# Encoder block: a refill's operations ordered behind lower parts of left operands, its first loads four products earlier, and the output weights' sums at other products

## The chip, the core and the metric

The kernel runs on one core of one Trainium2 chip. The metric is the device time of one execution in microseconds. In this core TensorE multiplies, VectorE (DVE) and ScalarE (ACT) work on tiles elementwise, GpSimd (POOL) does the same and issues some transfers, and SyncE (SP) issues most of the DMA transfers from one queue, in order. Each engine runs its instructions in the order in which the program gave them, and waits where an input is not there or a buffer is not free.

## The reference

One layer of an encoder block over 1040 positions (16 learned meta tokens and 1024 others), width 1024, all in float32: one input projection feeds a retention branch and a windowed attention branch, each with a gate and a projection of its own; the two are merged by sigmoid gates, projected once more, normed and added to the input.

```python
u = _rms_norm(h, pre_w)
z = u @ w_in
rq, rk, rv, rg, aq, ak, av, ag, gr, ga = _split_in(z)
...
o_r = o_r * ret_nw.astype(jnp.float32) * jax.nn.silu(rg.astype(jnp.float32))
y_r = o_r.astype(h.dtype) @ w_rb
...
o_a = _windowed_sink_attention(aq, ak, av, sink)[:, META_PAD:].reshape(B, T, ATT_Q)
o_a = o_a * jax.nn.silu(ag.astype(jnp.float32))
y_a = o_a.astype(h.dtype) @ w_ab

mix = jax.nn.sigmoid(gr) * y_r + jax.nn.sigmoid(ga) * y_a
out = mix @ w_o
return h + _rms_norm(out, post_w)
```

## The kernel before

**Precision.** A float32 operand is kept as two tiles: the upper part, cast by ScalarE (names in `h`), and the lower part, the operand less its upper part, made by VectorE in `dve_lo` (L92, names in `l`). A product of two operands is three matmuls in one accumulation (`mm3`, L76 to L78: upper by upper, lower by upper, upper by lower).

**Phases.** After the branches' projections, the retention and the attention come four matrix products, each an instance of `Phase`: z (the gate parts of the input projection, 16 units), r (`w_rb`), a (`w_ab`) and o (`w_out`), four units each. A unit is a strip of 256 columns of weights (phase o: of 256 positions) by 1024 in depth, and it is computed with seven block products in place of eight (the table `PROD`). A product is twelve matmuls with 512 columns: four pieces of the depth by three. The left operands are strips of weights, or sums of their blocks: raw strips `wrz<unit>_<half>` (`wrr`, `wra` in the other phases) are loaded, `prepare` makes the sums (`stz9S` and the like, L1006 and the lines around it), and `split` (L978, L92) casts them into `lhz<unit>_<product>` and `llz<unit>_<product>`, six buffers each. `prepare` runs six products ahead of the product that uses its result (`LEAD = 6`). Results are gathered in tiles `c1`, `u2`, `u3`, `c5` (L1068 is `plus`), multiplied, gated and stored in `z_post` (L1246 to L1260).

**The right operand.** It is kept in big buffers, for each phase the halves B11, T1, B21, B22 and the differences T2, T3, T4, each as an upper and a lower tile (`big0`, `big1`; `T30`, `T31`; `T40`, `T41`). Between two phases `refill` (L1142 to L1194) replaces it: it loads the next phase's matrix in tiles `z000` to `z113` (named for phase, row half, column half and piece; those of the refill behind phase r begin with r), makes differences of them (L1157), and splits each tile into its place as soon as the last product that reads that place is past. A table in `refill` gives each step the number of a product, counted from the end of the phase: at -17 the first loads, at -15 to -12 the first differences, at 0 to 10 the last splits (T3, B22, T4), which lie in the next phase already. A step is issued after the product of its number.

**The output weights' sums.** `pre_load` loads a quarter of `w_out` (`w00k`, `w01k`, `w11k`, `w10k`), and `pre_split` makes four differences of it (L776), casts them (`wT1hk` and so on), makes the lower parts (L92, `wT1lk`) and stores both parts to `preT` (L779, L781), for the refill behind phase a to fetch. `run` hooks them to products of the queue of all phases: the loads of quarter 0, 1, 2 and 3 behind product 16, 28, 40 and 52, the four sums 4, 6, 8 and 10 products later. Phase z has 92 products left at that point of the program, so all quarters lie in z, and the refill's first loads behind product 75.

**Order and buffers.** A scheduler in the framework lays out the instructions of each engine by modelled times and priorities; the order in which the code issues them is one input to it. `tc.issue_after(i)` adds an edge: what is issued under it stands behind instruction `i`. Loads and stores of all this (raw strips, refill, `preT`, gate values `tg_d`) share SP's queue. The staging tiles of the refill and of the sums share two pools: one of seven (the refill's left half-columns, and upper parts of the sums) and one of eight (the refill's right half-columns, the raw quarters and lower parts).

Of the kernel before, what the change touches and what calls it, by code (L numbers as in the profile page):

```python
# [39 lines left out]
def block_kernel(ctx: ExitStack, tc: tile.TileContext, x0, xT, x, meta, w_in, w_rb, w_ab, w_out, post_w,  # L40
# [50 lines left out]
    def dve_lo(o, i, hi):  # L91
        return nc.vector.tensor_tensor(o, i, hi.bitcast(F32), ALU.subtract).ins  # L92
# [19 lines left out]
    def halves_w(u):  # L112
        hi, lo = [], []

        def split(t, act):
            h, l = (wp.tile([P, 4, 256], R, tag=f"w{x}", bufs=4, name=f"w{x}{u}_{len(hi)}") for x in "hl")
            if act:
                nc.scalar.copy(h, t)
            else:
                pool_hi(h, t)  # L120
            hi.append(h)
            lo.append(l)
            return dve_lo(l, t, h)

        return split, ((lambda k, a, b: hi[k // 4][:, k % 4, a:b]), (lambda k, a, b: lo[k // 4][:, k % 4, a:b]))

    def load_w(src, u, act=False):
        split, w = halves_w(u)
        for t in fetch_w(src, u):
            split(t, act)  # L130
        return w
# [25 lines left out]
    def projT(w, c, name, mt=None):  # L157
        wh, wl = w
        a, b = cols(c)
        t = pj(name)  # L160
        if c == 0:
            for k in range(KT):
                nc.tensor.matmul(t[0:48, 0:256], xm[:, k, 0:48], wh(k, 0, 256), start=k == 0, stop=False,
                                 skip_group_check=True)
                nc.tensor.matmul(t[0:NM, 0:256], xm[:, k, 0:NM], wl(k, 0, 256), start=False, stop=k == KT - 1,
                                 skip_group_check=True)
            nc.scalar.copy(mt, t[32:32 + NM, 0:256])
            nc.vector.tensor_tensor(mt, t[0:NM, 0:256], mt, ALU.add)
            return mt
        for k in range(KT):  # L170
            mm3(t[0:b - a, 0:256], xh[k][:, a:b], xl[k][:, a:b], wh(k, 0, 256), wl(k, 0, 256), k == 0, k == KT - 1)
        return t
# [93 lines left out]
    with tc.tile_pool(name="setup", bufs=1, reuse_waits="tile") as st:  # L266
# [87 lines left out]
        split, wv0 = halves_w(U_V)  # L354
# [18 lines left out]
        first = [projT(wv0, 0, "pv0_0", vmeta0), projT(wv0, 1, "pv0_1"), projT(wv0, 2, "pv0_2")]  # L373
# [390 lines left out]
    def pre_load(k, src):  # L764

        w[k] = {}
        for i, j in ((0, 0), (0, 1), (1, 1), (1, 0)):
            w[k][i, j] = t = stage(f"w{i}{j}{k}", 1)
            src(t, 4 * i + k, j)

    def pre_split(k, i, behind):

        n, o, a, b = SUMS[i]
        x = w[k]
        with tc.issue_after(behind):
            nc.vector.tensor_tensor(x[o], x[a], x[b], ALU.subtract)  # L776
        h, l = (stage(f"w{n}{k}{e_}", s, R) for s, e_ in enumerate("hl"))
        nc.scalar.copy(h, x[o])
        nc.sync.dma_start(pre_d[n][0][:, k], h.bitcast(F32))  # L779
        dve_lo(l, x[o], h)  # L780
        nc.sync.dma_start(pre_d[n][1][:, k], l.bitcast(F32))  # L781
        if n == "T4":
            del w[k]

    w, near = {}, []
    gates = [U_G + u for u in range(4)] + [U_AG + u for u in range(4)] + [U_GR + u for u in range(8)]

    def pre_fetch(u):
# [157 lines left out]
    def stage(name, j=0, dt=F32):  # L946
        return (yp if j else lp).tile([P, 512], dt, tag=f"sg{int(j)}", bufs=8 if j else 7, name=name)
# [4 lines left out]
    def split_b(n, k, src):  # L952
        (h, as_), (l, _) = (right(n, s, k) for s in range(2))
        nc.scalar.copy(h, as_(src))
        dve_lo(l, as_(src), h)

    class Phase:
# [18 lines left out]
        def split(self, u, p, src):  # L976
            h, l = (lp.tile([P, 4, P], R, tag=t, bufs=LEAD, name=f"{t}{self.nm}{u}_{p}") for t in ("lh", "ll"))
            nc.scalar.copy(h, src)  # L978
            dve_lo(l, src, h)
            self.ops[u, p] = h, l  # L980

        def prepare(self, u, p):
# [147 lines left out]
    def get_pre(n):  # L1130
        for s in range(2):
            m = B[n][s].shape[1]
            nc.sync.dma_start(B[n][s].bitcast(F32), pre_d[n][s][:, 0:m])
            if m < 4:
                d, as_ = right(n, s, m)
                nc.sync.dma_start(d.bitcast(F32), as_(pre_d[n][s][:, m]))
# [8 lines left out]
    def refill(nm, src):  # L1145

        x = {}

        def load(i, j, ks=range(4)):
            def f():  # L1150
                for k in ks:
                    x[i, j, k] = t = stage(f"{nm}{i}{j}{k}", j)
                    src(t, 4 * i + k, j)
            return f

        def minus(o, a, b):
            return lambda k: nc.vector.tensor_tensor(x[*o, k], x[*a, k], x[*b, k], sub)  # L1157

        def split(n, i, j):
            return lambda k: split_b(n, k, x[i, j, k])  # L1160

        def each(at, n, *fs):
            for k in range(4):
                at.setdefault(n + k if len(fs) > 1 else n + k // 2, []).extend([lambda f=f, k=k: f(k) for f in fs])

        def got(n):
            return lambda: get_pre(n)

        def step(at, n, f):
            for k, j in enumerate(n):  # L1170
                at.setdefault(j, []).append(lambda k=k: f(k))

        if nm == "a":
            at = {-16: [load(0, 0)], -14: [load(1, 1)]}
            each(at, -13, split("B11", 0, 0))
            at.update({-11: [got("T1")], -10: [load(1, 0)], -9: [got("T2")], -5: [got("T3")], -1: [got("T4")]})
            each(at, -7, split("B21", 1, 0))
            each(at, -3, split("B22", 1, 1))
            return at

        at = {-17: [load(0, 0), load(0, 1)], -13: [load(1, 1)], -9: [load(1, 0, range(3))]}
        step(at, (-15, -14, -13, -12), minus((0, 1), (0, 1), (0, 0)))
        step(at, (-13, -12, -11, -10), split("B11", 0, 0))
        step(at, (-11, -10, -9, -8), split("T1", 0, 1))
        step(at, (-9, -8, -7, -6), minus((0, 1), (1, 1), (0, 1)))
        step(at, (-7, -6, -5, -4), split("T2", 0, 1))
        step(at, (-5, -4, -3, -2), minus((0, 0), (0, 1), (0, 0)))
        step(at, (-3, -2, -1, 3), split("B21", 1, 0))
        step(at, (-1, 0, 1, 3), minus((0, 1), (1, 0), (0, 1)))
        at[0].append(load(1, 0, (3,)))  # L1190
        step(at, (0, 1, 2, 4), split("T3", 0, 0))
        step(at, (4, 5, 6, 7), split("B22", 1, 1))
        step(at, (7, 8, 9, 10), split("T4", 0, 1))
        return at  # L1194

    def run(phases):

        jobs = [(ph, u, p) for ph, _ in phases for u, p in ph.seq]
        hooks, i = {}, 0
        for ph, src in phases:  # L1200
            i += len(ph.seq)
            if src:
                for j, f in refill(ph.nm, src).items():
                    hooks.setdefault(i + j, []).extend(f)

        for u in (0, 1):
            hooks.setdefault(len(jobs) - len(ph_o.seq) - 11 + u, []).insert(0, lambda u=u: ph_o.block(u, "A11"))
        for k in range(4):
            hooks[12 * k + 16] = [lambda k=k: pre_load(k, act_src(w_out))]
            for i in range(4):  # L1210
                hooks[12 * k + 20 + 2 * i] = [lambda k=k, i=i: pre_split(k, i, near[0])]
        n = 0
        for i, (ph, u, p) in enumerate(jobs):
            while n < min(i + LEAD, len(jobs)):
                q, u_, p_ = jobs[n]
                q.prepare(u_, p_)
                n += 1
            yield
            ph.product(u, p)
            for f in hooks.get(i, ()):  # L1220
                f()
# [6 lines left out]
    def act_src(d):  # L1228
        def src(o, k, j):
            nc.sync.dma_start(o, d[k, :, 512 * j:512 * j + 512])  # L1230
        return src
# [122 lines left out]
    def o_tail(o, a):  # L1354
# [4 lines left out]
        if a:  # L1359
            with tc.issue_after(scaled):  # L1360
                for c, t, _ in parts:
# [6 lines left out]
            (3, 4)]  # L1368
    ph_o = Phase("o", seq, o_load, o_post, apart=(0, 1))
    steps = run([(Phase("z", sequence(16, (1, 3, 2, 5, 6, 7, 4)), w_loader(w_in, gates), z_post, z_fetch,  # L1370
                        early=(0, 1), pre=PRE),
                  act_src(oTr_d)),
# [211 lines left out]
    i = attention()  # L1584
# [105 lines left out]
```

## Time and profile before

| | |
|---|---|
| time, median of 3 runs | 1039.8 us (1039.16 to 1040.24) |
| the profiled execution | 1040.69 us |
| its span | 1038.9 us |
| TensorE's mean granted clock | 0.996 |
| moved by DMA | 188.45 MB, mean 181 GB/s |

The span runs from the first to the last instruction of the profiled execution; the execution's own time is 1.8 us longer. Rows of the trace show the start in us, the duration, the engine, the line, the operation, and output<-inputs by the program's names; in square brackets stands how long the engine had waited and for what. Rows with a time pair `680.00:700.00` are windows: for each engine busy time and, in brackets, the number of instructions. Matmuls overlap, so the duration of one is longer than the distance between two.

### The profile page before, as it was taken

How to read it: one execution, taken by the hardware profiler on the slowest of the kernel's cores; microseconds unless marked ns; L12 is line 12 of the kernel's file. 1: busy time of each engine (PE TensorE's matmuls, PEld its weight loads, DVE VectorE, ACT ScalarE, POOL GpSimd, SP SyncE). 2: the span in 40 equal slices, each digit the busy share in tenths (PEclk: the TensorE clock that was granted, in tenths of full speed). 3: DMA queues.
4: the chain of work that ended last, by engine and by line, in shares of the span. 5: the costliest groups of instructions: out<-in, count | busy, mean ns of one | idle time of the engine just before them, and what ended most of it. 6: DMA issues, size and time to landing. Idle time of an engine off the chain costs nothing. (4 is left out here: it accounts for less than half of the span.)

```text
span 1038.9 us, 17321 instructions
## 1 busy us (share of the span) xinstructions
PE 1026.2 (99%) x5883; PEld 900.2 (87%) x5883; DVE 835.7 (80%) x1802; ACT 502.9 (48%) x1129; POOL 228.8 (22%) x368
## 2 busy tenths in 40 slices
PE   9999999999999999999999999999999999999997
PEld 8998999989989888988888888878888788888886
DVE  7786759768876778778769998999889889778665
ACT  5531432423423466664667554456466346334442
POOL 3445244243341433444310000000000000111042
PEclk9999999999999999999999999999999999999999
DMA  9433123243241466675659688999936656789463
GB/s 360 161 87 88 63 46 85 77 85 106 80 93 62 103 177 188 178 195 157 173 173 324 216 279 296 317 350 353 365 103 205 211 171 213 228 237 319 128 122 81
DMA packets 98840, 188.45 MB, mean 181 GB/s; under 512 B 13024, under 2 KB 37632, under 8 KB 98192
## 3 DMA queue, kind: packets, MB, share of 16 engines
q1 hardware_dynamic: 81200, 162.89, 46.6%
q0 software_dynamic: 10176, 14.73, 9.6%
q10 hardware_dynamic: 7376, 9.73, 2.7%
q8 instruction: 46, 0.75, 0.3%
q14 instruction: 42, 0.34, 0.1%
HBM read 124.32 MB, written 57.68 MB: 175 GB/s over the span
## 5 line engine op out<-in xcount | busy, mean ns | idle before, releaser
L1294 POOL DMA_DIRECT2D mx_d<-c1a x4 | 3.6, 890 | 396.4 <-DVE c1a L1285 396.4
L77 PE MATMUL bz<-big,llz 128*128 128x512 f32 x192 | 74.8, 390 | 0.2 <-DVE llz L92 0.2
L78 PE MATMUL bz<-big,lhz 128*128 128x512 f32 x192 | 74.2, 389 | 0.0
L76 PE MATMUL bz<-big,lhz 128*128 128x512 f32 x192 | 73.9, 389 | 0.0
L76 PE MATMUL pv<-wh,big 128*128 128x256 f32 x256 | 72.8, 284 | 0.0
L77 PE MATMUL pv<-wh,big 128*128 128x256 f32 x256 | 72.7, 284 | 0.0
L78 PE MATMUL pv<-wl,big 128*128 128x256 f32 x256 | 72.7, 284 | 0.0
L77 PE MATMUL bz<-T,llz 128*128 128x512 f32 x176 | 68.6, 390 | 0.6 <-DVE llz L92 0.6
L78 PE MATMUL bz<-T,lhz 128*128 128x512 f32 x176 | 68.5, 389 | 0.0
L76 PE MATMUL bz<-T,lhz 128*128 128x512 f32 x176 | 68.1, 390 | 0.3 <-DVE u2z L1068 0.3
L76 PE MATMUL paq<-big,wh 128*128 128x512 f32 x128 | 51.6, 403 | 0.0
L1434 ACT ACTIVATE p<-raw,nm 128x337 f32<-128x337 f32 (+1 forms) x64 | 35.5, 556 | 32.3 <-DVE nm L1431 30.9
L77 PE MATMUL paq<-big,wl 128*128 128x512 f32 x128 | 50.3, 393 | 0.0
L78 PE MATMUL paq<-big,wh 128*128 128x512 f32 x128 | 50.2, 392 | 0.0
L1447 POOL TENSOR_SCALAR p<-p,den 128x336 f32<-128x336 f32 (+2 forms) x60 | 34.6, 623 | 66.7 <-DVE den L1438 65.2
L76 PEld LDWEIGHTS pv<-wh,big 128*128 128x128 f32 x256 | 48.4, 189 | 0.4
L77 PEld LDWEIGHTS pv<-wh,big 128*128 128x128 f32 x256 | 48.3, 189 | 0.4
L78 PEld LDWEIGHTS pv<-wl,big 128*128 128x128 f32 x256 | 48.2, 188 | 0.3
L92 DVE TENSOR_TENSOR wl<-wr,wh 128x1024 fp32r<-128x1024 f32 x28 | 35.1, 1258 | 10.5 <-POOL wh L89 6.7
L77 PEld LDWEIGHTS bz<-big,llz 128*128 128x128 f32 x192 | 36.0, 188 | 7.9 <-DVE llz L92 0.5
L78 PEld LDWEIGHTS bz<-big,lhz 128*128 128x128 f32 x192 | 36.0, 188 | 7.5
L76 PEld LDWEIGHTS bz<-big,lhz 128*128 128x128 f32 x192 | 36.0, 188 | 7.4
(621 smaller groups left out, 3599.0 us busy)
## 6 DMA issues: line engine op xcount, KB each, us to landing
wrz<-in_w_in_dram SPq DMA_DIRECT2D x32, 512.0 KB, 6.1
wr<-in_w_in_dram SPq DMA_DIRECT2D x29, 512.0 KB, 3.9
we<-in_w_in_dram SPq DMA_DIRECT2D x16, 512.0 KB, 4.3
tg<-tg_d SPq DMA_DIRECT2D x32, 256.0 KB, 5.2
e<-e ACTq DMA_DIRECT2D x20, 256.0 KB, 2.6
e<-e SPq DMA_DIRECT2D x20, 256.0 KB, 5.2
xn<-in_x_dram SPq DMA_DIRECT2D x8, 512.0 KB, 9.1
oTr_d<-ost SPq DMA_DIRECT2D x16, 256.0 KB, 2.1
```

The source lines that it names most:

```text
L76: nc.tensor.matmul(o, ah, bh, start=first, stop=False, **kw)
L77: nc.tensor.matmul(o, al, bh, start=False, stop=False, **kw)
L78: latest[:] = [nc.tensor.matmul(o, ah, bl, start=False, stop=last, **kw).ins]
L92: return nc.vector.tensor_tensor(o, i, hi.bitcast(F32), ALU.subtract).ins
L1294: nc.gpsimd.dma_start(d, to, accum_op=ALU.add)
L1434: last["exp"] = nc.scalar.activation(pp[:, x_, w0 - o:w0 - o + 1 + wid], r[:, 0:1 + wid], AF.Exp, scale=-1.0, bias=nm_[:, x_:x_ + 1], accu ...
L1447: nc.gpsimd.tensor_scalar(v, v, den[:, x_:x_ + 1], 1.0, op0=ALU.mult, op1=ALU.mult)
```

## The change

Three things change. First, `split` records the instruction that makes a left operand's lower part, and in the refills behind phase z and phase r the first differences and the last splits are issued behind the newest one recorded (`behind`). The refill behind phase a is not touched. Second, in phase z the refill's first loads move from product -17 to -21 and the first differences from -15...-12 to -19...-16. Third, the loads of the output weights' quarters 1, 2 and 3 move from product 28, 40 and 52 to 27, 46 and 58, their sums with them.

```diff
--- before.py
+++ after.py
@@ -782,7 +782,7 @@
         if n == "T4":
             del w[k]
 
-    w, near = {}, []
+    w, near, ahead = {}, [], []
     gates = [U_G + u for u in range(4)] + [U_AG + u for u in range(4)] + [U_GR + u for u in range(8)]
 
     def pre_fetch(u):
@@ -976,7 +976,7 @@
         def split(self, u, p, src):
             h, l = (lp.tile([P, 4, P], R, tag=t, bufs=LEAD, name=f"{t}{self.nm}{u}_{p}") for t in ("lh", "ll"))
             nc.scalar.copy(h, src)
-            dve_lo(l, src, h)
+            ahead[:] = [dve_lo(l, src, h)]
             self.ops[u, p] = h, l
 
         def prepare(self, u, p):
@@ -1178,8 +1178,15 @@
             each(at, -3, split("B22", 1, 1))
             return at
 
-        at = {-17: [load(0, 0), load(0, 1)], -13: [load(1, 1)], -9: [load(1, 0, range(3))]}
-        step(at, (-15, -14, -13, -12), minus((0, 1), (0, 1), (0, 0)))
+        first = -21 if nm == "z" else -17
+        at = {first: [load(0, 0), load(0, 1)], -13: [load(1, 1)], -9: [load(1, 0, range(3))]}
+        def behind(f):
+            def g(k):
+                with tc.issue_after(ahead[0]):
+                    f(k)
+            return g
+
+        step(at, range(first + 2, first + 6), behind(minus((0, 1), (0, 1), (0, 0))))
         step(at, (-13, -12, -11, -10), split("B11", 0, 0))
         step(at, (-11, -10, -9, -8), split("T1", 0, 1))
         step(at, (-9, -8, -7, -6), minus((0, 1), (1, 1), (0, 1)))
@@ -1188,9 +1195,9 @@
         step(at, (-3, -2, -1, 3), split("B21", 1, 0))
         step(at, (-1, 0, 1, 3), minus((0, 1), (1, 0), (0, 1)))
         at[0].append(load(1, 0, (3,)))
-        step(at, (0, 1, 2, 4), split("T3", 0, 0))
-        step(at, (4, 5, 6, 7), split("B22", 1, 1))
-        step(at, (7, 8, 9, 10), split("T4", 0, 1))
+        step(at, (0, 1, 2, 4), behind(split("T3", 0, 0)))
+        step(at, (4, 5, 6, 7), behind(split("B22", 1, 1)))
+        step(at, (7, 8, 9, 10), behind(split("T4", 0, 1)))
         return at
 
     def run(phases):
@@ -1205,10 +1212,10 @@
 
         for u in (0, 1):
             hooks.setdefault(len(jobs) - len(ph_o.seq) - 11 + u, []).insert(0, lambda u=u: ph_o.block(u, "A11"))
-        for k in range(4):
-            hooks[12 * k + 16] = [lambda k=k: pre_load(k, act_src(w_out))]
+        for k, at in enumerate((16, 27, 46, 58)):
+            hooks[at] = [lambda k=k: pre_load(k, act_src(w_out))]
             for i in range(4):
-                hooks[12 * k + 20 + 2 * i] = [lambda k=k, i=i: pre_split(k, i, near[0])]
+                hooks[at + 4 + 2 * i] = [lambda k=k, i=i: pre_split(k, i, near[0])]
         n = 0
         for i, (ph, u, p) in enumerate(jobs):
             while n < min(i + LEAD, len(jobs)):
```

How the instructions come to stand on the engines is shown at three places. The rows have no times; they are an engine's order alone, and a number after a name's last underscore only tells one tile from another.

On VectorE in phase z, where units 8 and 9 are under way, before (`w102` is a difference of the output weights' third quarter, `wT22l` a lower part of it; `llz9_6` the lower part of a left operand):

```order
L1246 TENSOR_TENSOR c1z8_9066<-c1z8_9066,rbc_108 128x512
L1246 TENSOR_TENSOR c5z7_9042<-bz7_1_8809,rbc_108 128x512
L776 TENSOR_TENSOR w102_8856<-w102_8856,w112_8854 128x512
L92 TENSOR_TENSOR wT22l_9076<-w112_8854,wT22h_9075 128x512
L1259 TENSOR_TENSOR c5z6_9012<-c5z6_9012,v610_8858 128x512
L1246 TENSOR_TENSOR c1z9_9100<-c1z9_9100,rbc_108 128x512
L92 TENSOR_TENSOR llz9_6_9050<-stz9S_8991,lhz9_6_9049 128x512
```

The same place with the change:

```order
L1253 TENSOR_TENSOR c5z6_8997<-bz6_1_8781,rbc_108 128x512
L1079 TENSOR_TENSOR c1z8_9052<-c1z8_9052,e82_8894 128x512
L1253 TENSOR_TENSOR u3z7_8969<-u3z7_8969,rbc_108 128x512
L92 TENSOR_TENSOR wT12l_9106<-w002_9002,wT12h_9105 128x512
L92 TENSOR_TENSOR llz8_6_9013<-stz8S_8948,lhz8_6_9012 128x512
L92 TENSOR_TENSOR llz9_6_9036<-stz9S_8976,lhz9_6_9035 128x512
L92 TENSOR_TENSOR llz8_7_9063<-stz8S3_9060,lhz8_7_9062 128x512
```

Five of the quarter's operations that stood ahead of `llz9_6` now stand behind it, with the last of the eight, which stood behind it already; the last one ahead is `wT12l`.

On VectorE at the start of phase r, before (`big1<-z11...` is a split of B22, `r010` a difference of the next refill, `str1S` the sum that becomes the left operand of product 6):

```order
L92 TENSOR_TENSOR big1_113<-z110_9853,big0_112 128x512
L92 TENSOR_TENSOR llr1_5_10116<-str1S_10111,lhr1_5_10115 128x512
L1157 TENSOR_TENSOR r010_10460<-r010_10460,r000_10452 128x512
L92 TENSOR_TENSOR big1_113<-z111_9855,big0_112 128x512
L1068 TENSOR_TENSOR u2z15_9947<-u2z15_9947,bz15_5_9890 128x512
L92 TENSOR_TENSOR big1_113<-z112_9857,big0_112 128x512
L92 TENSOR_TENSOR big1_113<-z113_9859,big0_112 128x512
L1006 TENSOR_TENSOR str0S_10083<-str0S_10083,wrr0_0_10031 128x512
L1157 TENSOR_TENSOR r011_10462<-r011_10462,r001_10454 128x512
L1157 TENSOR_TENSOR r012_10464<-r012_10464,r002_10456 128x512
L1246 TENSOR_TENSOR u2z14_9925<-u2z14_9925,rbc_108 128x512
L1006 TENSOR_TENSOR str1S_10111<-str1S_10111,wrr1_0_10058 128x512
```

The same place with the change:

```order
L92 TENSOR_TENSOR llr1_5_10116<-str1S_10111,lhr1_5_10115 128x512
L1006 TENSOR_TENSOR str0S_10083<-str0S_10083,wrr0_0_10031 128x512
L1253 TENSOR_TENSOR u2z14_9925<-u2z14_9925,rbc_108 128x512
L1068 TENSOR_TENSOR u2z15_9947<-u2z15_9947,bz15_5_9890 128x512
L1006 TENSOR_TENSOR str1S_10111<-str1S_10111,wrr1_0_10058 128x512
L92 TENSOR_TENSOR llr0_6_10140<-str0S_10083,lhr0_6_10139 128x512
L1253 TENSOR_TENSOR u2z15_9947<-u2z15_9947,rbc_108 128x512
L1013 TENSOR_TENSOR str0S_10083<-wrr0_1_10084,str0S_10083 128x512
L92 TENSOR_TENSOR llr1_6_10164<-str1S_10111,lhr1_6_10163 128x512
L92 TENSOR_TENSOR T31_7803<-z000_9653,T30_7802 128x512
L92 TENSOR_TENSOR llr0_2_10191<-wrr0_1_10084,lhr0_2_10190 128x512
L92 TENSOR_TENSOR T31_7803<-z001_9655,T30_7802 128x512
```

The splits of T3 (`T31<-z00...`), B22 and T4 and the differences `r01...` stood ahead of the second `str1S` and now stand behind it, the first of them between the lower parts of the next left operands.

On SP's queue late in phase z, before (`wrz15_0` is a raw strip of the last unit, `c1z12`, `u3z11` and `c5z10` are stores of gate values):

```order
L1230 DMA z102_9953<-oTr_d_69 128x512
L1225 DMA wrz14_0_9675<-in_w_in_dram 128x1024
L1272 DMA tg0_100_10212<-tg_d_73 128x512
L1272 DMA tg0_011_10233<-tg_d_73 128x512
L1251 DMA tg_d_73<-c1z12_9586 128x512
L1251 DMA tg_d_73<-u3z11_9514 128x512
L1251 DMA tg_d_73<-c5z10_9541 128x512
L1225 DMA wrz15_0_9699<-in_w_in_dram 128x1024
```

The same place with the change:

```order
L779 DMA preT40_102<-wT43h_9586 128x512
L1237 DMA z001_9655<-oTr_d_69 128x512
L1237 DMA z002_9657<-oTr_d_69 128x512
L1237 DMA z003_9659<-oTr_d_69 128x512
L1237 DMA z010_9661<-oTr_d_69 128x512
L1237 DMA z011_9663<-oTr_d_69 128x512
L1258 DMA tg_d_73<-c5z11_9556 128x512
L781 DMA preT41_103<-wT43l_9587 128x512
L1237 DMA z012_9665<-oTr_d_69 128x512
L1237 DMA z013_9667<-oTr_d_69 128x512
L1258 DMA tg_d_73<-c1z13_9611 128x512
L1232 DMA wrz15_0_9716<-in_w_in_dram 128x1024
```

The refill's loads `z000` to `z013` and two stores of the output weights' last quarter now stand directly ahead of `wrz15_0`; before, the loads stood 16 to 26 rows ahead of it, with the later ones of the refill between. Where `wrz15_0` is used, on TensorE, before (`bz12` is the bank of unit 12, `bz13` of unit 13):

```order
L78 MATMUL bz13_1_9598<-T31_7803,lhz13_7_9619 128x512
L76 MATMUL bz12_1_9573<-T40_7804,lhz12_4_9636 128x512
L77 MATMUL bz12_1_9573<-T40_7804,llz12_4_9637 128x512
L78 MATMUL bz12_1_9573<-T41_7805,lhz12_4_9636 128x512
L76 MATMUL bz12_1_9573<-T40_7804,lhz12_4_9636 128x512
```

With the change:

```order
L78 MATMUL bz13_1_9598<-T31_7803,lhz13_7_9619 128x512
L78 MATMUL bz14_1_9821<-big1_113,lhz14_1_9693 128x512
L76 MATMUL bz15_1_9840<-big0_112,lhz15_1_9718 128x512
L77 MATMUL bz15_1_9840<-big0_112,llz15_1_9719 128x512
L76 MATMUL bz12_1_9566<-T40_7804,lhz12_4_9636 128x512
L77 MATMUL bz12_1_9566<-T40_7804,llz12_4_9637 128x512
```

Two matmuls of unit 15's first product, which use `lhz15_1` and `llz15_1` from `wrz15_0`, now stand ahead of unit 12's product 4.

## The prediction

> **What bounds the kernel now.** I read the page's head first, then a table of 20 us windows, then TensorE's own waits, then single rows at the places these point to.
>
> ```profile
> span 1038.9 us, 17321 instructions
> PE 1026.2 (99%) x5883; PEld 900.2 (87%) x5883; DVE 835.7 (80%) x1802; ACT 502.9 (48%) x1129; POOL 228.8 (22%) x368
> 680.00:700.00 20.00, 19.07 (x83) 15.13 (x83) 20.00 (x34) 9.94 (x17) 0.00 (x0) 1.00 0.97 333
> 700.00:720.00 20.00, 20.00 (x90) 16.57 (x89) 19.48 (x33) 13.04 (x23) 0.00 (x0) 1.00 0.98 363
> 720.00:740.00 20.00, 20.00 (x90) 16.57 (x89) 18.75 (x32) 10.26 (x18) 0.00 (x0) 1.00 0.97 345
> 740.00:760.00 20.00, 20.00 (x90) 16.53 (x90) 15.33 (x26) 8.42 (x15) 0.00 (x0) 1.00 0.82 291
> 760.00:780.00 20.00, 20.00 (x90) 16.57 (x89) 18.69 (x32) 14.69 (x27) 0.00 (x0) 1.00 0.26 93
> 800.00:820.00 20.00, 18.54 (x73) 14.43 (x72) 18.36 (x31) 9.73 (x19) 0.00 (x0) 0.91 0.70 230
> ```
>
> TensorE is the bound: busy 99% of the span, so only the places where its matmuls come late can be won back. In the windows (span, then busy time and count by engine, TensorE's clock, DMA share, GB/s) a full 20 us holds 90 matmuls; 680 to 700 holds 83 and 800 to 820 holds 73. VectorE is nearly as full: 34 operations in 680 to 700, without a pause. From 680 to 740 the DMA engines are at 97%; after 760 at 26%. TensorE's waits (total, times, longest) name who is late:
>
> ```profile
> PE br L76 <- ACT lhr L978: 1.4, 1, 1.4
> PE bz L77 <- DVE llz L92: 0.8, 2, 0.6
> 690.02 0.39 PE L78 MATMUL bz<-T,lhz 128*128 128x512 f32 x1
> 691.38 0.39 PE L78 MATMUL bz<-T,lhz 128*128 128x512 f32 x1
> 692.39 0.50 PE L77 MATMUL bz<-T,llz 128*128 128x512 f32 x1 [0.63 <-DVE llz L92]
> 692.73 0.39 PE L78 MATMUL bz<-T,lhz 128*128 128x512 f32 x1
> 694.80 0.39 PE L78 MATMUL bz<-T,lhz 128*128 128x512 f32 x1
> 695.49 0.47 PE L76 MATMUL bz<-T,lhz 128*128 128x512 f32 x1 [0.30 <-DVE u2z L1068]
> 695.80 0.39 PE L77 MATMUL bz<-T,llz 128*128 128x512 f32 x1
> 809.85 0.39 PE L76 MATMUL br<-T,lhr 128*128 128x512 f32 x1
> 811.66 0.51 PE L76 MATMUL br<-T,lhr 128*128 128x512 f32 x1 [1.42 <-ACT lhr L978]
> 813.04 0.62 PE L77 MATMUL br<-T,llr 128*128 128x512 f32 x1
> 816.44 0.41 PE L76 MATMUL br<-T,lhr 128*128 128x512 f32 x1
> ```
>
> Matmuls overlap, so I count from start to start: six steps from 690.02 to 691.38, 0.227 us each, and a product of twelve 2.72. Loss at the **first place**: 691.38 to 692.39 is 0.78 too long, the next step 0.11, 694.80 to 695.49 0.46, the next 0.08: **1.43 us**. **Second place**: 809.85 to 813.04 is four steps, 3.19 instead of 0.91: **2.28 us**. Then, from 813.04 to 816.44, eight steps take 3.40 instead of 1.81, 0.425 apiece: TensorE at half clock (the window's 0.91), **1.59 us**. The sum is 5.30 us of 1038.9.
>
> **What the change takes away.** At the first place the lower part that TensorE waits for stands behind sums of the output weights' third quarter:
>
> ```profile
> 689.25 0.68 DVE L776 TENSOR_TENSOR w<-w,w 128x512 f32<-128x512 f32 x1
> 689.85 0.68 DVE L92 TENSOR_TENSOR wT22l<-w,wT22h 128x512 fp32r<-128x512 f32 x1
> 691.66 0.68 DVE L92 TENSOR_TENSOR llz<-stz9S,lhz 128x512 fp32r<-128x512 f32 x1
> ```
>
> From 689.25 to 691.66 are four operations, 0.602 each: that is VectorE's price for one 128x512 operation here. The quarter has eight (4.82 us). Before, seven of them stand ahead of `llz9_6`; in the new order only `w002` and `wT12l` do, so five move behind it: 5 x 0.602 = 3.0 us sooner, against 0.78 and 0.46 of lateness. Gain 1.43. The moved ones are done while TensorE is in the products of units 8 to 11, where they displace work with a margin; the fourth quarter leaves 700 to 720 to make room and goes to 720 to 745, whose cover is VectorE's 4.7 idle us in 740 to 760.
>
> At the second place ScalarE casts the upper part `lhr1_6` as soon as VectorE has made `str1S`, and VectorE makes that behind the refill's last splits:
>
> ```profile
> 790.42 1.89 DVE L92 TENSOR_TENSOR T<-z,T 128x512 fp32r<-128x512 f32 x3
> 806.66 1.29 DVE L92 TENSOR_TENSOR big<-z,big 128x512 fp32r<-128x512 f32 x2
> 810.27 0.68 DVE L1006 TENSOR_TENSOR str1S<-str1S,wrr 128x512 f32<-128x512 f32 x1
> 810.99 0.62 ACT L978 CAST lhr<-str1S 128x512 fp32r<-128x512 f32 x1
> ```
>
> From 790.42 on twelve splits (four of T3, three and the margin of T4, four of B22) and three differences of the next refill stand before `str1S`; in the new order all fifteen stand after it, 15 x 0.602 = 9.0 us. Even if VectorE arrives there 5 us late (below), TensorE is served. Gain 2.28, and with the stall goes the half clock, 1.59. The splits' users are products 7, 3 and 4 of phase r, so nothing waits for them at once. The same tie in the refill behind phase r I cost at nothing: its operations only trade places in VectorE's queue, behind TensorE's products of phase r; uncovered it would cost one operation, 0.6. The second quarter's hook, 28 to 27, I cost at nothing for the same reason, with the same 0.6 if its cover were gone.
>
> **What it adds.** The refill's first loads (`z000` on) may run four products earlier by their step, but SP's queue has them behind the stores of the fourth quarter, and those come six products, 16.3 us, later. Behind the loads, in the same queue, stands `wrz15_0`, left operands of the last unit of phase z: eight z loads are between. When does it land?
>
> ```profile
> 712.30 0.32 SPq L995 DMA_DIRECT2D e<-e  x1
> 724.18 0.32 SPq L779 DMA_DIRECT2D preT<-wT43h  x1
> 741.75 0.45 SPq L1225 DMA_DIRECT2D wrz<-in_w_in_dram  x1
> DMA to landing us min/median/max: 6.5/6.9/7.0
> 750.25 0.62 ACT L978 CAST lhz<-wrz 128x512 fp32r<-128x512 f32 x1 [2.10 <-PE bz L78]
> 757.94 0.39 PE L76 MATMUL bz<-T,lhz 128*128 128x512 f32 x1
> ```
>
> The third row is `wrz15_0` before, landing 6.9 later (the `wrz` tile between 735 and 750), at 748.6; the cast at 750.25 waited for a buffer, which TensorE released. The needed time: in the new order TensorE's first matmul with `lhz15_1` stands one matmul behind the place that began at 757.94, so at 757.94 + 0.23 - 1.43 = 756.7, and with ScalarE's 0.62 and two short handovers `wrz15_0` must land by 756.0. The store `preT<-wT43h` moves from 724.18 to 724.18 + 16.3 - 1.43 = 739.1. Behind it come eleven issues. Their pace: 24 issues from 724.18 to 741.75, 0.73 each; or, slower, twelve from 712.30 to 724.18, 0.99 each. So issue at 747.1 to 750.0, and 1.5 later still if the store waits as it does in a full queue: landing **754.0 to 758.5**, a stall of 0 to 2.5 us. I take the middle, 756.3: 0.3, and, as at the first place, 0.5 for the weak restart and the lower part that follows the upper: **0.80 us**.
>
> VectorE is hit harder. Its queue is strict, and `llz15_1` waits in it for the same cast; behind it stand the refill's differences, the sums of units 14 and 15 and all splits. So the idle of 740 to 760 falls before 756 and is no cover afterwards. From `llz15_1` to `llz15_4` are 57 operations in the new order, 34.3 us without one pause, and 0.75 until the last is visible; TensorE has 147 matmuls between its first use of `lhz15_1` and `llz15_4`, 33.3 us and the 0.5 above. 35.05 - 33.85 = **1.2 us** of stall near 792, 0.05 more for the restart: **1.25**. In the old trace the same two stand 37.1 us apart, pauses included, and began early enough:
>
> ```profile
> 750.91 0.69 DVE L92 TENSOR_TENSOR llz<-wrz,lhz 128x512 fp32r<-128x512 f32 x1
> 788.02 0.68 DVE L92 TENSOR_TENSOR llz<-wrz,lhz 128x512 fp32r<-128x512 f32 x1
> ```
>
> If the weights land early by some time, this stall shrinks by as much: its bounds are 0 and 1.3.
>
> **Sum.** -5.30 + 0.80 + 1.25 = -3.25. On the profiled execution, 1038.9 becomes 1035.65, and with the 1.8 around it (1040.69) 1037.4. The median of the runs, 1039.8, is 0.9 below that execution: 1036.5.
>
> **A rule on the clock.** In the trace a stretch of 3.19 us with four matmuls in it, its longest start-to-start 1.81, was followed by 3.40 us at half clock; the first place, 1.24 lost in 4 us, was not. The Trainium skill, "TensorE: Matmul & The Clock Gate", section "Why this matters for your kernels", puts the limit at idle gaps over about 3 us between bursts. By that rule no stall of mine could cost clock, and rival 1 below would end at 1038.0; the trace disagrees with it at 813.04, and the row decides.
>
> **Rivals.**
> 1. *The weights land at the late bound, and the clock falls.* 2.5 + 0.1 of stall at 757 is as much idle as the second place had, so 1.59 of half clock follows, and 1.25 near 792: 5.44 against 5.30. Time 1039.9, no change. For it: DMA is at 97% for 60 us before, and the loads of z are packed. Against: the new order takes the third and fourth quarters' traffic out of 680 to 715, so the queue should be shorter than the old rows.
> 2. *Slower: the queue is longer than any old row.* If every transfer from 735 on lands 1 us later, fourteen issues with about eight under way cost two such delays before `wrz15_0` is issued, one more at its landing: 758.5 + 3 = 761.5, stall 5.5, clock 1.59, VectorE 1.25, so 8.3 - 5.3 = +3.0: 1042.8. It decides from a landing at 758.7 on. For it: DMA share that leaves no reserve. Against: the share falls to 0.82 and 0.26 behind 740, so there is room for moved bytes.
> 3. *Nothing is added.* The weights land at 754: 1039.8 - 5.3 = 1034.5.
> 4. *The tie does not free the second place*, because VectorE comes there late with its own backlog: 2.28 and 1.59 stay, -1.43 + 2.05 = +0.6: 1040.4. Against: 9.0 us less ahead of `str1S`.
>
> **How the numbers follow.** About 0.2% (2.1 us) is what a measurement of this kernel tells from no change. The forecast, with rival 3 as its better end, has 0.65 (time 1034.5 to 1038), rival 1 0.21, rival 2 0.09, rival 4 0.05. Nearly all of the first is faster by over 2.1 us, 0.62; the rest of it, rival 1 and rival 4 are within it, 0.29; slower 0.09. Range: from rival 3 with a little beneath it, 1034.2, to rival 1, 1039.9.
>
> **What would show it.** 90 matmuls in 680 to 700 and no wait on `llz` there; no TensorE row above 0.3 us between 800 and 816 and a clock of 1.00; a wait of TensorE on ScalarE's `lhz` near 757, with a VectorE pause of 3 to 5 us that ends with it; a wait on `llz` near 792. SP issuing `z000` near 740 rather than 721. Wrong would be a stall over 3 us near 757, half clock behind it, late weights of units 10 to 13, or any TensorE wait in phases r or a.

## The result

The changed kernel takes 1036.5 us (median of 7 runs, 1035.8 to 1038.4) against 1039.9 beside it (7 runs, 1039.2 to 1043.3): a ratio of 0.9964, interval 0.9951 to 0.9977. A second run of it gave 1036.2 against 1040.4, 0.9961 (0.9949 to 0.9973). The forecast was 1036.5.

The head of the page after, and the 20 us windows (span, then busy time and count by engine, TensorE's clock, DMA share, GB/s) at the places that the prediction speaks of:

```profile
span 1034.4 us, 17323 instructions
680.00:700.00 20.00, 20.00 (x90) 16.57 (x89) 18.46 (x31) 10.25 (x18) 0.00 (x0) 1.00 0.91 304
740.00:760.00 20.00, 20.00 (x90) 16.57 (x89) 14.64 (x24) 6.55 (x12) 0.00 (x0) 1.00 0.99 347
780.00:800.00 20.00, 20.00 (x89) 16.34 (x88) 20.00 (x35) 14.59 (x27) 0.00 (x0) 1.00 0.48 153
800.00:820.00 20.00, 20.00 (x90) 16.55 (x89) 18.54 (x32) 10.37 (x19) 0.00 (x0) 1.00 0.70 227
```

680 to 700 holds 90 matmuls where it held 83, and 800 to 820 holds 90 where it held 73, at full clock. The DMA share is lower from 680 to 740 (0.91, 0.92 and 0.78 by window, where it was 0.97 to 0.98), and the fullest stretch is now 740 to 760 (0.99, where it was 0.82). The profiled execution took 1036.18 (span 1034.4 and the same 1.8 around it).

The 4.5 us between the two spans are not the change's alone. TensorE, VectorE and ScalarE have the same orders in both kernels until behind 630 us, where the second quarter's sums differ, yet phase z did not begin at the same time. The first late row of phase z in the timeline, before, and the same one after:

```profile
546.44 0.50 PE L77 MATMUL bz<-big,llz 128*128 128x512 f32 x1 [0.17 <-DVE llz L92]
```
```profile
547.46 0.50 PE L77 MATMUL bz<-big,llz 128*128 128x512 f32 x1 [0.23 <-DVE llz L92]
```

In the 14 executions profiled for this study this row begins between 546.40 and 547.76, so over a microsecond is decided ahead of it by equal instructions. I therefore count **from this row to the span's end**: 492.46 us before, 486.94 after. The change's own part in these two executions is -5.5.

What the prediction added did not come. After, in the order of time: SP's issues, ScalarE's cast of `wrz15_0`, VectorE's lower part, TensorE's first use of it, then `llz15_4` and its users:

```profile
740.74 0.41 SPq L779 DMA_DIRECT2D preT<-wT43h  x1
748.03 1.68 SPq L1232 DMA_DIRECT2D wrz<-in_w_in_dram  x3
755.36 0.62 ACT L978 CAST lhz<-wrz 128x512 fp32r<-128x512 f32 x1 [3.47 <-DMA wrz<-in_w_in_dram]
756.01 0.69 DVE L92 TENSOR_TENSOR llz<-wrz,lhz 128x512 fp32r<-128x512 f32 x1 [3.47 <-ACT lhz L978]
757.68 0.39 PE L76 MATMUL bz<-big,lhz 128*128 128x512 f32 x1
790.31 0.68 DVE L92 TENSOR_TENSOR llz<-wrz,lhz 128x512 fp32r<-128x512 f32 x1
791.05 0.50 PE L77 MATMUL bz<-T,llz 128*128 128x512 f32 x1
791.38 0.40 PE L78 MATMUL bz<-T,lhz 128*128 128x512 f32 x1
```

The cast waited 3.47 us for the transfer and VectorE paused 3.47 us with it, as forecast (3 to 5). But the cast was done 1.7 us ahead of TensorE's use. From `llz15_1` to `llz15_4` VectorE needed 34.30 us, which is 57 x 0.602 within 0.02, and `llz15_4` arrived as TensorE came to it: 0.1 us lost in the row behind. The place had no time left over.

At the first place, VectorE's `llz9_6` after; it stood at 691.66:

```profile
684.55 0.68 DVE L92 TENSOR_TENSOR llz<-stz9S,lhz 128x512 fp32r<-128x512 f32 x1
```

The second place after: VectorE's `str1S` for product 6, the first of the tied splits, and TensorE's first row of product 6.

```profile
803.53 0.68 DVE L1006 TENSOR_TENSOR str1S<-str1S,wrr 128x512 f32<-128x512 f32 x1
806.55 0.68 DVE L92 TENSOR_TENSOR T<-z,T 128x512 fp32r<-128x512 f32 x1
809.54 0.39 PE L76 MATMUL br<-T,lhr 128*128 128x512 f32 x1
```

`str1S` stands at 803.53 in place of 810.27, the splits behind it, and TensorE shows no late row from 800 to 820.

### The profile page after: what moved, and what is told of

It reads as the page before. It is cut to its first block, busy times and chain, and to the rows that moved or that the text cites. A ratio compares the mean times of both kernels' runs of the same rounds, so it can differ in the third digit from the quotient of the medians.

```text
span 1034.4 us, 17323 instructions
## 1 busy us (share of the span) xinstructions
PE 1022.7 (99%) x5883; PEld 898.5 (87%) x5883; DVE 833.0 (81%) x1802; ACT 501.9 (49%) x1129; POOL 227.9 (22%) x368
```

## The experiments

All are compared with the kernel before on the same chip, in five rounds; "from z" is the time from the row named above to the end of the span. The last column leaves out 0.2 us near 890 in four of the runs, of which more below. Profiles that lose at most 0.1 behind z take 486.7 to 486.9 from z, so the last column, with 1.6 for a half clock, accounts for the one before it.

| run | us | ratio to before (95%) | from z | late rows of TensorE behind z in its profile |
|---|---|---|---|---|
| before | 1039.9 | 1 | 492.5 | 1.43 at 692, 2.28 + 1.59 at 811 |
| the change | 1036.5 | 0.9964 (0.9951-0.9977) | 486.9 | 0.1 at 791 |
| `same` | 1036.2 | 0.9961 (0.9949-0.9973) | 487.4 | 0.6 at 943 |
| `e1_tie` | 1038.2 | 0.9967 (0.9954-0.9980) | 489.3 | 0.9 at 638, 1.6 at 694 |
| `e2_hooks` | 1041.1 | 1.0002 (0.9992-1.0011) | 491.5 | 3.1 at 811, then half clock |
| `e3_early` | 1040.7 | 0.9989 (0.9978-1.0000) | 493.4 | 0.4 at 637, 1.9 at 694, 2.3 at 813, then half clock |
| `e4_tie_hooks` | 1036.6 | 0.9954 (0.9938-0.9969) | 487.9 | 1.0 at 792 |
| `e4_again` | 1036.1 | 0.9956 (0.9943-0.9970) | 488.9 | 1.1 at 638, 0.9 at 792 |
| `d4` | 1036.5 | 0.9966 (0.9953-0.9979) | 486.7 | 0.1 at 791 |
| `d8` | 1039.0 | 0.9990 (0.9982-0.9999) | 491.6 | 1.4 at 638, 0.6 at 772, 1.3 at 787, 1.2 at 791 |
| `e9_tie_splits` | 1039.0 | 0.9994 (0.9981-1.0007) | 490.6 | 3.8 at 753 |
| `e10_tie_first` | 1039.4 | 0.9990 (0.9980-1.0000) | 489.3 | 0.6 at 807, 1.4 at 811 |
| `h28` | 1036.2 | 0.9953 (0.9940-0.9967) | 486.8 | none |
| `v57` | 1036.0 | 0.9957 (0.9942-0.9971) | 487.3 | 0.5 at 791 |

**The three parts, alone and in pairs.** From the changed kernel, `e1` keeps the tie alone, `e2` the hooks alone, `e3` the early loads alone, `e4` tie and hooks:

```diff
# e1, e2, e4
-        first = -21 if nm == "z" else -17
+        first = -17
# e1, e3
-        for k, at in enumerate((16, 27, 46, 58)):
+        for k, at in enumerate((16, 28, 40, 52)):
# e2, e3, likewise at the three last splits
-        step(at, range(first + 2, first + 6), behind(minus((0, 1), (0, 1), (0, 0))))
+        step(at, range(first + 2, first + 6), minus((0, 1), (0, 1), (0, 0)))
```

> The tie of the refills alone; the output weights' sums at their old products (28, 40, 52) and the refill's first loads at -17. Theory A (each place has its own cause: the third quarter's sums make the first place late, the refill's last splits the second): the second place goes with its half clock, 2.28 + 1.59 = 3.87 us, and the first stays with its 1.43; from 1039.9 to about 1036.0, with TensorE's wait on llz near 692 still in the trace and none near 811. Theory B (the second place is a backlog that the earlier loads remove): no change, 1039.9, and the wait on lhr near 811 stays. Theory C (the sums' place decides both, since it loads DMA and VectorE together): no change or under 1 us, 1039 to 1039.9.

> The sums of quarters 1 to 3 at products 27, 46 and 58 alone; no tie, first loads at -17. Theory A: the first place goes (1.43), the second stays and may grow, since the fourth quarter's sums now push VectorE's later work (0 to 2 us): 1038.5 to 1040.5, wait on lhr near 810 of 1.4 us or more. Theory B: 1038.5 as well, with the same wait. Theory C: 1036.0 to 1036.5, no wait near 810.

> The refill's first loads at -21 and its first differences at -19 to -16 alone; no tie, sums at 28, 40 and 52. Theory A: nothing is taken away from either place, 1039.5 to 1040.2. Theory B: the second place goes, 1036.0. Theory C: as before, 1039.9.

> The change without its earlier loads: tie, sums at 27, 46 and 58, first loads at -17. Theory A with the loads as a mere load on SP's queue ahead of wrz15_0: wrz15_0 lands several us sooner, both old places are gone, so the same time as the change or a little less, 1035.5 to 1036.5. Rival D (the loads had to come earlier, because the fourth quarter now fills VectorE where the refill's first differences stood, and without it the lower part of unit 15's product 4 is late by about 1 us near 791): 1037 to 1038.

With the tie alone only the first place is left of the two:

```profile
694.07 0.50 PE L77 MATMUL bz<-T,llz 128*128 128x512 f32 x1 [0.75 <-DVE llz L92]
697.17 0.47 PE L76 MATMUL bz<-T,lhz 128*128 128x512 f32 x1 [0.31 <-DVE u2z L1068]
```

With the hooks alone the first place is gone and the second has grown from 2.28 to 3.1, with the half clock behind it (0.43 us between matmuls from 813.54 on):

```profile
811.90 0.50 PE L76 MATMUL br<-T,lhr 128*128 128x512 f32 x1 [1.90 <-ACT lhr L978]
813.54 0.63 PE L77 MATMUL br<-T,llr 128*128 128x512 f32 x1
813.97 0.63 PE L78 MATMUL br<-T,lhr 128*128 128x512 f32 x1
```

So each place has its own cause, as theory A has it; theories B (the early loads remove the second) and C (the sums decide both) fall. `e1` gained 3.1 us beside the kernel before, less than the 3.87 expected: the half clock is not in every execution (next section). The hooks alone are worth nothing in time: they win the 1.43, but the second place costs 0.85 more and the half clock, by the mean granted clock, came in 10 of 12 executions where the kernel before had it in 11 of 24, an estimated 0.6 more. That it is the fourth quarter's move that makes the second place worse was expected, and no run tried it alone. The early loads alone take nothing away from either place; the interval of `e3`'s ratio reaches 1.0000.

Without the early loads (`e4`, twice) TensorE waits on `llz15_4` near 792, 1.0 and 0.9 us: rival D's mechanism, with VectorE's pause now for `wrz14_1` and longer, 4.90 us:

```profile
757.55 0.69 DVE L1004 TENSOR_TENSOR stz14S<-wrz,wrz 128x512 f32<-128x512 f32 x1 [4.90 <-DMA wrz<-in_w_in_dram]
792.23 0.50 PE L77 MATMUL bz<-T,llz 128*128 128x512 f32 x1 [0.75 <-DVE llz L92]
```

Yet its times are not worse than the change's (0.9954 and 0.9956). What the early loads are worth stays open: up to 1 us by the two profiles, nothing by the runs.

> Tie and sums without the earlier loads, once more. If the wait of 0.9 us on llz15_4 near 792 that its first execution showed is its rule: the same wait again and 1037.0 to 1037.6. If it comes and goes with the landing of wrz14_1: a wait between 0 and 1 us, 1036.0 to 1036.8, no difference from the change.

**Which half of the tie.** `e9` ties the last splits alone, `e10` the first differences alone.

```diff
# e9
-        step(at, range(first + 2, first + 6), behind(minus((0, 1), (0, 1), (0, 0))))
+        step(at, range(first + 2, first + 6), minus((0, 1), (0, 1), (0, 0)))
# e10, likewise for B22 and T4
-        step(at, (0, 1, 2, 4), behind(split("T3", 0, 0)))
+        step(at, (0, 1, 2, 4), split("T3", 0, 0))
```

> The change with the tie on the last splits alone: the first differences are free and stand ahead of llz15_1 on VectorE, where they wait for the refill's loads. If the tie on the differences matters (VectorE held up by z013 ahead of llz14_1 and llz15_1): a wait of 1 to 2.5 us near 750 to 758, 1037.5 to 1039. If not (VectorE pauses there for wrz15_0 anyway, so a pause for z013 ahead of it costs nothing): 1036.0 to 1037.0, and no wait above 0.3.

> The change with the tie on the first differences alone, the last splits free. Theory A (the second place is the last splits ahead of str1S): it comes back, 2.28 us and in a part of the executions 1.6 of half clock: 1038.4 to 1040.2 where the change takes 1036.3, with a wait on lhr near 811. Rival H (the tie's worth is all on the first differences, since without it there the run beside the change was 2.8 us slower): 1036.0 to 1037.0, no wait near 811.

Both lose most of the gain. In `e10` the second place is back, with 2.0 us lost in two waits, on the lower parts this time, and no half clock; the longer one:

```profile
811.55 0.50 PE L77 MATMUL br<-T,llr 128*128 128x512 f32 x1 [1.16 <-DVE llr L92]
```

In `e9` a place appears that neither kernel has. VectorE's pause ahead of the first difference, and the matmul that waited for the sum queued behind it:

```profile
751.06 1.29 DVE L1157 TENSOR_TENSOR z<-z,z 128x512 f32<-128x512 f32 x2 [4.32 <-DMA tg_d<-c5z]
752.27 0.68 DVE L1068 TENSOR_TENSOR u2z<-e,bz 128x512 f32<-128x512 f32 x1
753.00 0.50 PE L76 MATMUL bz<-T,lhz 128*128 128x512 f32 x1 [3.53 <-DVE u2z L1068]
```

The releaser of the pause is named as a store that lies directly behind the loads `z000` to `z011` in SP's queue; that store lands at 752.62, when the pause is over, so one of those loads is likelier. Four differences stand ahead of `llz15_1` in that order, the first two ahead of the `u2z` that frees unit 12's bank. It takes later sums and earlier differences together: `e3`, with the early differences untied but the sums at their old products, has no pause there, and in `e2`, with the later sums and the differences untied at their old products, the first difference waits 1.84 us at 750.35 and TensorE is on time. The reading that fits is that the loads stand behind the sums' stores in SP's queue and come late for the early differences; the tie puts these behind the operand that TensorE needs next.

**A later landing.** `d4` and `d8` put four and eight more stores of a constant tile on SP's queue ahead of `wrz15_0` (the edit of `d4`; the line that reserves `extra_d` is left out here, and `d8` has 8 in place of 4):

```diff
-        nc.sync.dma_start(pre_d[n][1][:, k], l.bitcast(F32))
+        d = nc.sync.dma_start(pre_d[n][1][:, k], l.bitcast(F32)).ins
+        if n == "T4" and k == 3:
+            with tc.issue_after(d):
+                for m in range(4):
+                    nc.sync.dma_start(extra_d[m], rbc[:, half[0]])
```

> The change with four more stores of 128x512 (of a constant tile, into memory that nothing reads) on SP's queue ahead of wrz15_0, which lands later by their issue, 4 x 0.61 = 2.4 us by the pace of the 14 issues from 739.48 to 748.03. Theory E (VectorE's pause for wrz15_0 ends later by as much, nothing of it can be made up in the 57 operations behind, and llz15_4 was at its edge): TensorE loses 2.4 us in all between 757 and 795, 0.7 to 1.2 of it near 757 and the rest on llz15_4: 1038.5 to 1039.2 against 1036.5. Rival F (there is slack, or stores beside the loads cost no time): 1036.0 to 1037.0.

> As before with eight more stores: 8 x 0.61 = 4.9 us later. Theory E: 4.9 us lost between 757 and 795, 3.2 or more of it near 757, and with over 2.3 us of idle there half clock for 1.6 us behind it: 1041 to 1043. Rival F: 1036 to 1038.

`d4` moved the landing as worked out, counted from the row at z's start: the cast began 207.9 us behind that row in the change, 210.3 in `d4`. The time did not move, so theory E fell as it stood:

```profile
757.28 0.62 ACT L983 CAST lhz<-wrz 128x512 fp32r<-128x512 f32 x1 [4.25 <-DMA wrz<-in_w_in_dram]
757.94 0.69 DVE L93 TENSOR_TENSOR llz<-wrz,lhz 128x512 fp32r<-128x512 f32 x1 [3.46 <-ACT lhz L983]
```

The scheduler saw the stores and laid the two engines out anew: TensorE's two matmuls of unit 15 moved back behind nine matmuls of unit 12's product 4, and 53 operations in place of 57 were left between `llz15_1` and `llz15_4`. TensorE's use thus comes 2.0 us later, beside the 1.7 that the cast had in hand, and the stretch is 2.4 us shorter, just the delay. So a later landing at a fixed order remains untried. `d8`'s landing is 6.7 us later, not the 4.9 expected; of this 3.2 reached TensorE, 0.6 at 772 and the rest where no theory had it, on ScalarE's copies of `u3` behind casts of the refill:

```profile
787.32 0.50 PE L77 MATMUL bz<-T,lhz 128*128 128x512 f32 x1 [1.05 <-ACT u3z L1070]
791.63 0.50 PE L77 MATMUL bz<-T,lhz 128*128 128x512 f32 x1 [0.98 <-ACT u3z L1070]
```

**Neighbours and the repeat.** `h28` puts the second quarter back to product 28, `v57` the fourth to 57 (the tuple of the hooks is the whole edit).

> The changed kernel once more, as the measure for the runs beside it and for how much its executions differ: 0.9951 to 0.9977 of the kernel before again. If the place near 757 to 792 is at its edge (no slack left in the first profile), this execution may show a wait on llz near 792 of 0 to 1.5 us, as long as wrz15_0 lands later than 7.8 us after TensorE's first matmul 210 us into phase z did in the first; if there is slack, none.

> The change with the second quarter's sums at product 28 again. If that move is worth nothing, as costed: 1035.9 to 1036.8, and TensorE's rows near 638 to 655 as in the change. Rival (at 28 the second quarter holds up ScalarE or VectorE near 638, where two runs with 28 showed TensorE 0.3 and 0.8 us late and one with 27 showed 1.3): 1036.8 to 1037.8.

> The change with the fourth quarter at product 57 in place of 58, its stores 2.7 us sooner ahead of wrz15_0. If the place from 757 to 792 still costs the change something in its middle execution: 1035.3 to 1036.0, and VectorE's pause ahead of llz15_1 ends 2 us sooner. If the change has nothing left to win there: 1035.9 to 1036.8.

All three give the change's time. `same` is the equal program with the equal orders, yet TensorE lost 0.6 us in phase a, where the prediction had named any wait as a sign against it:

```profile
942.93 0.50 PE L76 MATMUL ba<-big,lha 128*128 128x512 f32 x1 [0.35 <-DVE u3a L1068]
```

No other profile has this wait, and its cause stays open. In `v57` VectorE's pause ended 0.6 us sooner than in the change, counted from z's row, not the 2 expected; 58 operations stand behind it up to `llz15_4`, and 0.5 was lost on that. The second quarter's move is worth nothing; the waits near 638 come and go with either number (28 in `e1` and `e3`, 27 in `e4_again` and `d8`, none with 28 in `h28`), so they are not the hook's. None of the neighbours can be told from the change, and no version here is shown to beat it.

## Why the prediction was right, point by point

The two places and their causes were right, and so was the direction. That the time came out to a tenth is luck: two terms that were not paid (2.05 us) and one that the median did not have to give back (1.59) nearly cancel.

**First place, 1.43: right.** It stays at 1.6 in `e1` and goes in `e2`, by the hooks, as said. `llz9_6` came 8.1 us sooner, counted from z's row, where the five moved operations had been 3.0; the new layout put other operations behind it too.

**Second place, 2.28: right.** It goes in `e1` and is back with 2.0 in `e10`: the last splits ahead of `str1S`. In the change `str1S` came 7.8 us sooner, counted from z's row, of the 9.0 worked out. Rival 4 fell.

**Half clock, 1.59: mechanism right, size wrong for the median.** The first profile had it, so the sum took it away whole. Beside `e1` to `e4` the kernel before ran 24 times: in 11 the mean granted clock was 0.996 or 0.997 (median 1042.45), in 13 it was 0.998 (1040.7). In the two later rounds it was so in 8 of 23 and 6 of 17, with medians 1.2 and 0.5 apart. So the middle execution does not pay it. None of the 12 executions of the change in its two runs is below 0.998. The prediction had in hand that its profiled execution was 0.9 above the median, and did not ask why. By the two places alone, 1039.9 - 3.7 = 1036.2; the change takes 1036.5 and, in the second run, 1036.2. Rival 1 without its half clock, given as 1038.0, is 1039.9 - 1.59 = 1038.3 by its own terms.

**Late weights, 0.80: the step "I take the middle" failed.** `preT<-wT43h` was issued at 740.74, 193.3 us behind the row at z's start, where the prediction put it at 192.7. The eleven issues behind it took 7.29 us, 0.66 each, a little under the quick bound of 0.73; the store did not wait the 1.5 us that I added. `wrz15_0` landed near the lower bound: the cast that waited for it began 207.9 us behind z's row, 754.3 on the old time, where the middle had been 756.3. The rows that gave the slow pace were no measure of the queue: from 712.30 to 724.18 SP waited for VectorE and ScalarE, and for no transfer. The two longest of these waits (total, times, longest):

```profile
SPq L779 <- ACT wT43h L778: 1.8, 1, 1.8
SPq L1225 <- DVE llz L92: 1.7, 2, 1.5
```

The DMA share does not order the paces: it was 0.90 in these slow rows, 0.99 in the quick ones up to 741.75 and 0.92 during the eleven issues of the change.

**VectorE's saturated stretch, 1.25: the working was exact, its start was not.** 57 operations, 34.3 us and no pause, as worked out. With the landing 2 us sooner than the middle it ended in time, as the text said it would ("this stall shrinks by as much"). That the stretch decides is seen in `e4`, where the pause ended 1.3 us later, counted from z's row, and 1.0 was lost on the same lower part.

**The tie on the first differences** was priced nowhere: I counted them among VectorE's 57 operations and missed that untied they hold up a bank (`e9`, 3.8 us). It was part of what made the forecast come true, unforeseen.

**The tie behind phase r, nothing:** the kernel before lost 0.2 us at 890, and so do `e2`, `e3` and `e10`, where the last splits are free; `e1` and the change lose nothing there. A gain of two tenths that I left out.

**Rivals 1 and 2** (a landing from 758.5 on, on the old time) did not come; `d8` landed that late, with another layout, and lost neither their 2.5 us near 757 nor the clock. Rival 3, nothing added, is what the traces show; its 1034.5 was too low by the half clock that the median does not have.

## What to carry to other kernels

Before a stall's price is taken off the median, ask whether the median execution pays it: a profile that stands above the median may have something that the others have not. Where a queue's pace is taken from old rows, see first what the queue waited for in them: a stretch in which it waits for other engines tells nothing of its own pace. And a tie on an operation that must wait for a load is worth what stands behind it on its engine, not its own duration.

## What the runs showed of the hardware

The clock fell in some executions of an equal program and not in others, by the mean granted clock: 11 of 24 above, 10 of 12 in `e2`, where 3.1 us are lost. Where a profile shows it, it stayed at half for 3.41 us: from 813.04 to 816.45 in the kernel before, 812.87 to 816.29 in `e2`, 814.59 to 818.00 in `e3`. It falls once more at each execution's end, when TensorE is done: at 1034.91, 1034.74 and 1036.46. In all three that is 64 times 3.413 us after the clock had come back. So in each execution the clock changes on a grid of 3.413 us.

The length of an idle stretch alone does not decide. In `e9`'s profile no matmul began for 3.9 us,

```profile
749.09 0.39 PE L76 MATMUL bz<-big,lhz 128*128 128x512 f32 x1
753.00 0.50 PE L76 MATMUL bz<-T,lhz 128*128 128x512 f32 x1 [3.53 <-DVE u2z L1068]
```

and the clock stayed full there (five of `e9`'s other eleven executions have a mean clock of 0.996 or 0.997, so in those it seems to have fallen), while in the kernel before 2.28 us lost in a stretch of 3.19, with matmuls between, halved it. The grid tells the two apart. These are the steps of the grid just ahead of the fall in the kernel before, in `e2` and in `e3`, and then the two steps over which `e9`'s gap lies, counted back from its own last fall at 1034.72 (span, then busy time and count for TensorE, its weight loads, VectorE, ScalarE and GpSimd, clock, DMA share, GB/s):

```profile
809.63:813.04 3.41, 1.95 (x6) 0.86 (x5) 3.41 (x7) 2.65 (x5) 0.00 (x0) 1.00 0.79 277
809.46:812.87 3.41, 1.49 (x4) 0.56 (x3) 3.41 (x7) 2.24 (x5) 0.00 (x0) 1.00 0.97 311
811.18:814.59 3.41, 1.94 (x7) 0.98 (x6) 3.41 (x7) 3.02 (x6) 0.00 (x0) 1.00 0.82 275
748.00:751.42 3.42, 1.48 (x7) 0.90 (x5) 0.36 (x1) 0.00 (x0) 0.00 (x0) 1.00 0.92 300
751.42:754.83 3.41, 1.82 (x8) 1.52 (x9) 3.41 (x7) 0.00 (x0) 0.00 (x0) 1.00 1.10 383
```

In the first three the idle time lies within one step; in `e9` the longer gap is shared by two. Counted at 0.227 us for each matmul from its start (an estimate), matmuls fill 1.1, 0.7 and 1.1 us of the first three steps and 1.3 and 1.7 of `e9`'s. In all 14 profiles, behind z's row, every step filled to 1.13 us or less is followed by half clock, and none filled to over 1.4. The Trainium skill, "TensorE: Matmul & The Clock Gate", section "What's actually happening", tells of a free-running window of 3413 ns in which activity is judged. The 3.41 us at half clock, the grid and the lottery between executions agree with it. How the grid lay in the executions without a trace is not known, and no run moved it on purpose.
